# All operands at multiples of 128 bytes in SBUF: a pad behind the constants and wider slots in a two-layer diffusion trunk

## The chip, the cores and the metric

One core of one Trainium2 chip runs the whole kernel as one program. The metric is the device time in microseconds. The profile is one execution, recorded by the hardware profiler.

## The reference

Two layers work on 640 tokens of 1024 features: 128 prompt tokens and 512 latent ones. All data are float32. Each layer is a feed-forward, a mixer and a second feed-forward, each with its modulated norm and a gated residual:

```python
def swiglu(h, w_in, w_out):                      # w_in (1024, 5632), w_out (2816, 1024)
    gt, up = jnp.split(h @ w_in, 2, axis=-1)
    return (jax.nn.silu(gt) * up) @ w_out

def ffn_sublayer(x, mod, g, w_in, w_out, slot):
    h = pre_norm(x, g, mod[:, 3 * slot], mod[:, 3 * slot + 1])
    return x + 0.5 * mod[:, 3 * slot + 2] * swiglu(h, w_in, w_out)

# layer 0: x += gate * concat(conformer_conv(u), hgrn2(u)) @ w_out, u = pre_norm(x) @ w_in
# layer 1: x += gate * windowed attention with a sink logit, QK norm and 2-D rotary
```

The modulation comes from `silu(cond) @ w_mod + b`, with one condition for the prompt tokens and one for the latent ones.

## The kernel before

Activations lie feature-major: `x` is `[128 partitions, 8, 640 tokens]`, so a tile of 128 features is 640 float32 values per partition. The tokens are split in two chunks (`CHUNKS`), first tokens 384 to 639 (256 columns), then tokens 0 to 383 (384 columns).

Every large matrix product is made by `product_steps` (line L531 of the profile). A float32 operand is split into two float32r parts: a rounded one (`hi`, a cast on ScalarE, L517) and the rest (`lo`, a subtraction on VectorE, L518). For each of the contraction's tiles of 128 there are three products, `hi*hi`, `hi*lo` and `lo*hi`, which sum in one PSUM bank. TensorE loads 128 columns of weights for each (LDWEIGHTS, the profile's PEld) and streams 256 or 384 columns of the activations past them (MATMUL).

```python
terms = ((whi, xhi), (whi, xlo), (wlo, xhi))
for j, (a, b) in enumerate(terms):
    self.last_mm = nc.tensor.matmul(ps, lhsT=a[k], rhs=b[k][:, c0:c0 + n], ...
```

In a feed-forward (`ffn`) there are 22 tiles of 128 hidden features, in parts of 8, 8 and 6. A tile takes two products over 8 contraction tiles (gate and value, `pg` and `pu` in the profile), a part ends with a product into the 8 output tiles (`po`, in `project_out`). The mixers use the same routine for their 34 projections (`pj_...`), and their output projection is made in two halves of 4 tiles, with the same `po`; their operand is then called `m`. The attention's scores (L1210, `as`) are float32r products too.

SBUF is given out by pools, one after the other, in this order: the constants (`const`), `x` (`xp`), 6 raw weight tiles (`raw`), 3 + 3 split weight tiles `whi`/`wlo` (`w`), then `slots`, scratch (`tmp`) and `small`. The pool `slots` holds 12 slots of 640 columns, 6 wide ones (`N_WIDE`, 685 columns, for the conv's padded input) and 16 pairs, each of two tiles of 640. The norm's output `h`, the hidden features `g` and the mixers' `m` are pairs, hi and lo side by side; these are the operands that TensorE streams. Weights of the start of the next phase, or of the last output tiles before a norm (`wg`, `wu`, `o` without hi and lo in the profile's names), are split into slots instead, narrow or wide.

Each tile is rounded up to a multiple of 32 bytes per partition, and begins where the one before it ends.

Of the kernel before, what the change touches and what calls it, by code (L numbers as in the profile page):

```python
# [8 lines left out]
F32 = mybir.dt.float32  # L9
# [7 lines left out]
P = 128  # L17
# [3 lines left out]
T = TP + TS  # L21
# [9 lines left out]
WIDE = T + 45  # L31
AHEAD = 400
# [34 lines left out]
class Trunk:  # L67
# [21 lines left out]
    def pair(self, name, dtype=F32):  # L89
        """two tiles of T columns side by side, [P, 2, T], until free(name)"""  # L90
        assert name not in self.held, name
        j = self.free_pairs.pop(0)
        self.held[name] = ("pair", j)
        return self.slots.tile([P, 2, T], dtype, tag=f"pair{j}", name=name)

    def two(self, name, dtype):
        """the two parts of a value"""
        if self.free_pairs:
            t = self.pair(name, dtype)
            return t[:, 0], t[:, 1]  # L100
        self.held[name] = ("two", None)
        return self.slot(f"{name}hi", dtype), self.slot(f"{name}lo", dtype)

    def slot(self, name, dtype=F32, n=T):
        """a tile of T columns until free(name): a slot, or half of a pair; with self.spread_out the one that has been
        free for longest"""
        assert name not in self.held, name
        if n > T:
            j = next(j for j in self.free_slots if j < N_WIDE)
            self.free_slots.remove(j)  # L110
            self.held[name] = ("slot", j)
            return self.slots.tile([P, WIDE], dtype, tag=f"slot{j}", name=name)[:, :n]
        never = float("inf")
        halves = [x for x in self.halves if x[2] == dtype]
        age = {"half": self.freed["half", halves[0][0], halves[0][1]] if halves else never,
               "slot": self.freed["slot", self.free_slots[0]] if self.free_slots else never,
               "pair": self.freed["pair", self.free_pairs[0]] if self.free_pairs else never}
        order = ("slot", "half", "pair")
        if self.spread_out:
            order = sorted(order, key=age.get) if dtype == F32 else ("slot", "half", "pair")  # L120
            if dtype == F32 and len(self.free_slots) <= KEPT:
                order = sorted(("half", "pair"), key=age.get) + ["slot"]
        kind = next(k for k in order if age[k] < never)
        if kind == "slot":
            j = next((j for j in self.free_slots if j >= N_WIDE and not self.spread_out), self.free_slots[0])
            self.free_slots.remove(j)
            self.held[name] = ("slot", j)
            return self.slots.tile([P, WIDE if j < N_WIDE else T], dtype, tag=f"slot{j}", name=name)[:, :n]
        if kind == "half":
            half = halves[0]  # L130
            self.halves.remove(half)
        else:
            j = self.free_pairs.pop(0)
            t = self.slots.tile([P, 2, T], dtype, tag=f"pair{j}", name=name)
            half = (j, 0, dtype, t)
            self.halves.append((j, 1, dtype, t))
            self.freed["half", j, 1] = self.freed["pair", j]
        self.held[name] = ("half", half)
        return half[3][:, half[1], :n]
# [22 lines left out]
    def banks(self, n_mm, n_acc=0, n_mod=0):  # L162
        """the eight PSUM banks: for products, for sums held over several steps, for the modulation, for the rest"""
        n_aux = 8 - n_mm - n_acc - n_mod
        self.bank, b = {}, 0
        for kind, n in (("mod", n_mod), ("mm", n_mm), ("acc", n_acc), ("aux", n_aux)):
            self.bank[kind] = list(range(b, b + n))
            b += n
# [17 lines left out]
    def plan(self, n, points, skip):  # L186
        """the next n fillers go to the next so many points"""
        points -= skip
        self.points = [0] * skip + [-(-n * (p + 1) // points) + (-n * p // points) for p in range(points)]
# [34 lines left out]

    def vec_block(self, b):
# [24 lines left out]
    def transpose_x(self, rows):  # L250
        """x feature-major, and 1 / sqrt(mean square + eps) by token on all partitions"""
# [26 lines left out]
    def conditions(self):  # L278
        """conditions after silu, by feature"""
# [10 lines left out]
    def mod_piece(self, l, slot, q):  # L290
        """256 of the modulation's features; the contraction in four parts that run side by side on columns of the
        array"""
# [18 lines left out]
    def mod_step(self, l, slot, k):  # L311
        """one of eight steps of a whole slot: products with the conditions summed by partition, over the steps by
        VectorE and at the end over the partitions by TensorE, a quarter of the features by part of the array"""
# [51 lines left out]
    def square_into(self, k, c):  # L365
        """squares of a tile summed into acc; the last tiles' stay apart"""
# [17 lines left out]
    def rstd(self, sq_tiles, blocks, scale_col, eps, name, eng=None):  # L384
        """1 / sqrt(mean + eps) by token, tokens on partitions: [P, len(blocks)]; tiles with their first tokens"""
# [16 lines left out]
    def inv_root(self, r, x, scale, name, eng=None):  # L402
        """r = scale / sqrt(x), x > 0: a guess from the exponent, a Newton step and one of third order (1e-9)"""
# [26 lines left out]
    def spread(self, col, out):  # L430
        """a value by token (on partitions) to all partitions: out [P, 128 tokens]"""
        self.nc.tensor.transpose(out, col.to_broadcast([P, P]), self.ident)
# [54 lines left out]
    def split_w_slots(self, raw, name):  # L487
        """the same with the parts in slots, until free(name)"""
# [34 lines left out]
    def product_steps(self, ps, w, x, c0, n):  # L523
        """ps += w.T @ x, float32 operands as exact sums of two float32r parts"""
# [11 lines left out]
    def ffn_first(self, l, which, j):  # L536
        """the weights of a tile of hidden features, for the gate and for the value, with names"""
# [3 lines left out]
    def prefetch(self):  # L541
        """weights of the next phase's start, into slots"""
# [48 lines left out]
    def project_out(self, w, xhi, xlo, n, final, last=False):  # L591
        """x += gate * (w.T @ x); the last tiles before a norm run chunk by chunk, which hides the norm's start"""
# [52 lines left out]
    def root_table(self, after):  # L645
        """has the square root's table loaded ahead"""
# [21 lines left out]
    def project(self, w_ap, name, fine=False):  # L668
        """one tile of 128 features: yields (psum, first token, tokens), and None in between"""
# [11 lines left out]
    def project_tokens(self, w_ap, dst, name):  # L681
        """256 features, token-major, block by block; dst(block): (output, first feature, features) to copy"""
# [18 lines left out]
    def even_constants(self):  # L701
# [20 lines left out]
        # forget gate lb + (1 - lb) * sigmoid(z) as lb_mid + lb_half * tanh(z / 2)  # L722
# [3 lines left out]
        # the conv's gate is 2 * sigmoid(z) = 1 + tanh(z / 2)  # L726
# [3 lines left out]
    def conv_tile(self, ct, w, by_chunk=False):  # L730
        """the gated input of 128 channels: prompt and sample, with 15 zeros before, between and after"""
# [43 lines left out]
    def front(self, ins, n):  # L775
        """counts DVE time; the instruction is one that taps may follow"""
        self.marker = ins
        self.dve_time += n + 60

    def background(self, last=False):  # L780
        """taps for the time that DVE has left while TensorE works on what is emitted so far"""
# [7 lines left out]
    def tick(self):  # L789
        """after a chunk of products: next steps of the scan and of the conv's norm, queued behind them, and taps"""  # L790
# [82 lines left out]
    def hgrn_scan(self, h, qf, gates):  # L873
        """steps of a head's scan"""
# [9 lines left out]
        # scores, transposed: A[s, block, t]; the levels replace all of a block but its diagonal  # L884
# [14 lines left out]
        for lv in range(LEVELS):  # L899
# [3 lines left out]
            def mixed(a, b0, nb):  # L903
                """of pairs of runs of w: the first from a[:, 0] and the second from a[:, 1]"""
# [32 lines left out]
        # states: prompt f, b; sample f after blocks 0..2, b after blocks 3..1  # L937
# [120 lines left out]
    def mix_out(self, w, n, k0, k1, names):  # L1058
        """the part of the output projection that reads tiles k0 to k1 of the mixer's output"""
# [15 lines left out]
    def rope(self, x, name):  # L1075
        """rotates the sample tokens of x in place"""
# [17 lines left out]
    def odd_values(self, w):  # L1094
        """values token-major: prompt, sample blocks 0..3, cache, two blocks in a slot"""
# [7 lines left out]
    def odd_keys(self, w, i, fine=False):  # L1103
        """two heads: parts of the keys, each on both halves of the partitions, for sample blocks 0, 1, the cache
        and sample blocks 2, 3; the prompt's apart"""
# [51 lines left out]
    def head_squares(self, ps, t0, n, r, name):  # L1157
        """mean square + eps by token, for both heads of the 128 features in ps: r[:, 2 * block + head]"""
# [10 lines left out]
    def odd_queries(self, w, i):  # L1169
# [13 lines left out]
        # per head both parts stacked on the partitions: [hi; lo] and [lo; hi]  # L1183
# [9 lines left out]
    # first key column, key columns, first band column, value blocks, by query block  # L1193
# [3 lines left out]
    def attend_scores(self, i, b):  # L1197
        """exp(scores - maximum) of two heads' queries in a block, and the terms of their sums"""
# [33 lines left out]
    def attend_turn(self, i, b):  # L1232
        """keys to the partitions"""
# [32 lines left out]
    def attend_sums(self, i):  # L1266
        """divides by the sums of both heads"""
# [168 lines left out]
```

## Time and profile before

| | us |
|---|---|
| median of 3 runs | 2555.15 (2554.66 to 2556.28) |
| span of the profiled execution | 2550.6 |
| TensorE busy in it | 2503.3 |
| VectorE busy | 1513.1 |
| ScalarE busy | 815.9 |
| GpSimd busy | 193.1 |

The profiled execution's span, from its first to its last instruction, lies 4.6 us below the median of the timed runs; the rest is outside the span. A matmul's record is longer than the distance to the next one, since they are pipelined. Their pace is therefore read from start to start.

### The profile page before, as it was taken

The numbers are of one execution on the slowest core, as the hardware profiler recorded it, in microseconds if no ns is written. First come the engines' busy times: TensorE is split into PE (matmuls) and PEld (weight loads), VectorE is DVE, ScalarE is ACT, GpSimd is POOL, SyncE is SP. The second block draws the span as 40 slices with busy tenths as digits, with TensorE's granted clock in tenths as the row PEclk, the third lists the DMA queues.
The fourth block names the chain that finished last, engine by engine and source line by source line (L and its number), as shares of the span: only waits on it lengthen the run. The fifth ranks groups of instructions, "written<-read, shape, count | busy, mean of one in ns | idle before, by whom it ended". The sixth has DMA issues, their size and how long they took to land. (4 is left out here: it accounts for less than half of the span.)

```text
span 2550.6 us, 42680 instructions
## 1 busy us (share of the span) xinstructions
PE 2503.3 (98%) x17802; PEld 2440.3 (96%) x17802; DVE 1513.1 (59%) x2733; ACT 815.9 (32%) x1519; POOL 193.1 (8%) x282
## 2 busy tenths in 40 slices
PE   8999999999989999999999999999999999999999
PEld 5999999999989999999999999999988899999999
DVE  6765665569987766455556544545667863333333
ACT  5222212443234422221233212223465642222121
POOL 0000000124143000000010000000122010000000
PEclk9999999999999999999999999999999999999999
DMA  8654444311211344344433433433200122222221
GB/s 279 186 157 133 139 143 136 105 53 54 61 32 42 94 124 142 107 133 133 122 103 101 132 108 108 124 106 118 59 19 15 42 84 68 82 75 75 83 63 54
DMA packets 368522, 254.50 MB, mean 100 GB/s; under 512 B 8789, under 2 KB 350152, under 8 KB 368328
## 3 DMA queue, kind: packets, MB, share of 16 engines
q1 hardware_dynamic: 363384, 248.35, 32.3%
q10 hardware_dynamic: 4944, 3.41, 0.4%
q8 instruction: 140, 2.29, 0.4%
q14 instruction: 54, 0.44, 0.1%
HBM read 248.32 MB, written 3.41 MB: 99 GB/s over the span
## 5 line engine op out<-in xcount | busy, mean ns | idle before, releaser
L531 PE MATMUL po<-g,whi_o 128*128 128x256 f32 (+1 forms) x2672 | 573.4, 307 | 0.0
L531 PE MATMUL pg<-h,whi_wg 128*128 128x256 f32 (+1 forms) x2656 | 572.5, 307 | 0.0
L531 PE MATMUL pu<-h,whi_wu 128*128 128x256 f32 (+1 forms) x2656 | 568.2, 306 | 0.3 <-DVE nt L456 0.3
L531 PEld LDWEIGHTS po<-g,whi_o 128*128 128x128 f32 x2672 | 442.7, 188 | 3.7 <-ACT whi_o L517 1.2
L531 PEld LDWEIGHTS pg<-h,whi_wg 128*128 128x128 f32 x2656 | 441.3, 188 | 2.9 <-issue 2.5
L531 PEld LDWEIGHTS pu<-h,whi_wu 128*128 128x128 f32 x2656 | 439.9, 188 | 0.6 <-issue 0.6
L325 DVE SCALAR_TENSOR_TENSOR ma<-raw_wm,cond,ma 128x512 f32<-128x512 f32 x448 | 316.6, 747 | 205.2 <-DMA raw_wm<-in_w_mod 205.1
L531 PE MATMUL po<-g,wlo_o 128*128 128x256 f32 (+1 forms) x1336 | 408.5, 306 | 0.0
L531 PE MATMUL pg<-h,wlo_wg 128*128 128x256 f32 (+1 forms) x1328 | 406.8, 306 | 0.0
L531 PE MATMUL pu<-h,wlo_wu 128*128 128x256 f32 (+1 forms) x1328 | 405.8, 306 | 0.0
L605 DVE SCALAR_TENSOR_TENSOR x<-po,modG,x 128x256 f32<-128x256 f32 (+1 forms) x384 | 156.5, 435 | 240.3 <-PE po L531 239.3
L531 PEld LDWEIGHTS po<-g,wlo_o 128*128 128x128 f32 x1336 | 250.8, 188 | 0.0
L531 PEld LDWEIGHTS pg<-h,wlo_wg 128*128 128x128 f32 x1328 | 250.2, 188 | 0.0
L531 PEld LDWEIGHTS pu<-h,wlo_wu 128*128 128x128 f32 x1328 | 249.3, 188 | 0.0
L517 ACT CAST whi_o<-raw_o 128x1024 fp32r<-128x1024 f32 (+3 forms) x113 | 104.4, 924 | 385.7 <-PE po L531 246.2
L575 DVE TENSOR_TENSOR sil<-sil,pu 128x256 f32<-128x256 f32 (+1 forms) x176 | 85.3, 485 | 204.5 <-PE pu L531 200.7
L517 ACT CAST g<-sil 128x256 fp32r<-128x256 f32 (+1 forms) x176 | 80.4, 457 | 307.7 <-DVE sil L575 307.6
L518 DVE TENSOR_TENSOR wlo_wu<-raw_wu,whi_wu 128x1024 fp32r<-128x1024 f32 x83 | 101.5, 1223 | 119.3 <-ACT whi_wu L517 119.3
L517 ACT CAST whi_wg<-raw_wg 128x1024 fp32r<-128x1024 f32 x83 | 87.3, 1051 | 255.4 <-issue 130.7
L517 ACT CAST whi_wu<-raw_wu 128x1024 fp32r<-128x1024 f32 x83 | 87.2, 1050 | 216.8 <-PE pg L531 167.0
L382 POOL TENSOR_TENSOR acc<-acc,sq 128x256 f32<-128x256 f32 (+1 forms) x44 | 41.9, 954 | 1442.7 <-ACT sq L381 1442.5
L518 DVE TENSOR_TENSOR wlo_o<-raw_o,whi_o 128x1024 fp32r<-128x1024 f32 (+3 forms) x113 | 121.5, 1075 | 30.7 <-ACT whi_o L517 28.6
(412 smaller groups left out, 3470.5 us busy)
## 6 DMA issues: line engine op xcount, KB each, us to landing
raw_wm<-in_w_mod SPq DMA_DIRECT2D x144, 512.0 KB, 3.6
raw_wg<-in_ffn_w_in SPq DMA_DIRECT2D x88, 512.0 KB, 3.8
raw_wu<-in_ffn_w_in SPq DMA_DIRECT2D x88, 512.0 KB, 4.0
raw_o<-in_ffn_w_out SPq DMA_DIRECT2D x64, 512.0 KB, 4.1
raw_o<-in_ffn_w_out SPq DMA_DIRECT2D x32, 384.0 KB, 3.5
raw_z<-in_ev_w_in SPq DMA_DIRECT2D x8, 512.0 KB, 3.8
raw_oq<-in_od_w_in SPq DMA_DIRECT2D x8, 512.0 KB, 3.7
raw_o<-in_od_w_out SPq DMA_DIRECT2D x16, 256.0 KB, 2.7
```

The source lines that it names most:

```text
L325: nc.vector.scalar_tensor_tensor(out=acc, in0=part, scalar=col, in1=acc, op0=ALU.mult, op1=ALU.add)
L382: nc.gpsimd.tensor_tensor(out=self.acc[:, c0:c0 + n], in0=self.acc[:, c0:c0 + n], in1=sq[:, 0:n], op=ALU.add)
L517: nc.scalar.copy(out=hi, in_=src)
L518: nc.vector.tensor_tensor(out=lo, in0=src, in1=hi.bitcast(F32), op=ALU.subtract)
L531: self.last_mm = nc.tensor.matmul(ps, lhsT=a[k], rhs=b[k][:, c0:c0 + n], start=(k == 0 and j == 0), stop=(k == nk - 1 and j == 2))
L575: nc.vector.tensor_tensor(out=s, in0=s, in1=pu, op=ALU.mult)
L605: nc.vector.scalar_tensor_tensor(out=xs, in0=ps[:, s0 - c0:s0 - c0 + sn], scalar=self.modG[:, n, m, g:g + 1], in1=xs, op0=ALU.mult, op1=AL ...
```

## The change

24 float32 values (96 bytes) are given out at the end of the constants and never used. A wide slot becomes 704 columns (2816 bytes) instead of 685 (2740, rounded up to 2752); what is read and written in it stays as long as before. The rest of the difference is blank lines in the place of comments.

```diff
+WIDE_ROOM = 704
...
-            return self.slots.tile([P, WIDE], dtype, tag=f"slot{j}", name=name)[:, :n]
+            return self.slots.tile([P, WIDE_ROOM], dtype, tag=f"slot{j}", name=name)[:, :n]
...
-            return self.slots.tile([P, WIDE if j < N_WIDE else T], dtype, tag=f"slot{j}", name=name)[:, :n]
+            return self.slots.tile([P, WIDE_ROOM if j < N_WIDE else T], dtype, tag=f"slot{j}", name=name)[:, :n]
...
         self.modG = c.tile([P, 6, KD, 2], F32, name="modG")
 
+        c.tile([P, 24], F32, name="pad")
```

No instruction moves on any engine: the rows of both programs are the same, and so are their waits. The first byte per partition of the tiles, in the two built programs, modulo 128:

| tiles | before | after |
|---|---|---|
| `ident` (streamed in transposes) | 0 | 0 |
| `x`, `raw`, `whi`, `wlo`, 12 narrow slots, scratch | 32 | 0 |
| 6 wide slots | 32, 96, 32, 96, 32, 96 | 0 |
| 16 pairs (`h`, `g`, `m`) | 96 | 0 |

A tile of 128 weight columns is 512 bytes, a pair's half 2560 and the first chunk's start inside a tile 1536 bytes, all of them multiples of 128. So an operand of a product has the remainder of its tile.

## Rows read from the trace of the kernel before

**Rows 1.** The page's first part: busy us (share of the span) x instructions.
```profile
PE 2503.3 (98%) x17802; PEld 2440.3 (96%) x17802; DVE 1513.1 (59%) x2733; ACT 815.9 (32%) x1519; POOL 193.1 (8%) x282
```

**Rows 2.** The waits: engine, line, what released it: us in total, times, longest.
```profile
PE hgb L432 <- DVE r_hg L414: 9.9, 3, 6.4
...
DVE x L605 <- PE po L531: 239.3, 139, 3.7
```

**Rows 3.** Stretches A:B of the span, line L531 alone: busy us (instructions), clock, DMA.
```profile
100.00:480.00 380.00, 373.25 (x2579) 370.30 (x2578) 1.00 0.46 140
...
1340.00:1790.00 450.00, 444.59 (x3084) 441.99 (x3083) 1.00 0.38 115
```

**Rows 4.** Order in time, TensorE, first feed-forward: start us, us, line, tiles, count.
```profile
300.51 0.51 PE L531 MATMUL pg<-h,whi_wg 128*128 128x384 f32 x2
300.86 0.34 PE L531 MATMUL pg<-h,wlo_wg 128*128 128x384 f32 x1
301.03 0.51 PE L531 MATMUL pg<-h,whi_wg 128*128 128x384 f32 x2
301.38 0.34 PE L531 MATMUL pg<-h,wlo_wg 128*128 128x384 f32 x1
301.55 0.51 PE L531 MATMUL pg<-h,whi_wg 128*128 128x384 f32 x2
301.90 0.34 PE L531 MATMUL pg<-h,wlo_wg 128*128 128x384 f32 x1
302.07 0.51 PE L531 MATMUL pu<-h,whi_wu 128*128 128x384 f32 x2
```

**Rows 5.** Order in time, TensorE, 256 columns in the same stage.
```profile
306.23 0.39 PE L531 MATMUL pg<-h,whi_wg 128*128 128x256 f32 x2
...
307.25 0.39 PE L531 MATMUL pg<-h,whi_wg 128*128 128x256 f32 x2
```

**Rows 6.** Order in time, TensorE: transposes of the scan, products of the conv's norm.
```profile
611.38 1.04 PE L950 MATMUL kt<-ident,k 128*128 128x128 f32 x8
...
748.91 1.84 PE L815 MATMUL cmu<-cw,ones_c 128*128 128x399 f32 x5
```

**Rows 7.** The same lines' views: duration ns min/median/max, first and last start, forms.
```profile
L950 PE MATMUL kt<-ident,k x32: 270/272/273, 611.4 to 823.7; 128*128 128x128 f32 x32
...
L815 PE MATMUL cmu<-cw,ones_c x16: 377/440/501, 746.5 to 756.3; 128*128 128x399 f32 x8, 128*128 128x256 f32 x8
```

**Rows 8.** Order in time, TensorE, attention scores.
```profile
1875.75 0.33 PE L1210 MATMUL as<-khi,qs 128*128 128x384 f32 x1
...
1876.46 0.34 PE L531 MATMUL pj_oq<-h,whi_oq 128*128 128x384 f32 x1
...
2021.97 0.34 PE L1210 MATMUL as<-khi,qs 128*128 128x384 f32 x1
...
2022.67 0.50 PE L531 MATMUL po<-m,whi_o 128*128 128x384 f32 x2
```

**Rows 9.** Order in time, TensorE, a norm's sums: one column streamed.
```profile
510.89 0.58 PE L391 MATMUL rs_n<-ones_d,apart 128*128 128x1 f32 x4
511.33 0.36 PE L391 MATMUL rs_n<-ones_d,acc 128*128 128x1 f32 x2
511.56 0.47 PE L391 MATMUL rs_n<-ones_d,apart 128*128 128x1 f32 x3
```

**Rows 10.** Order in time, TensorE, output tiles after the even mixer, two windows.
```profile
853.42 0.76 PE L531 MATMUL po<-m,o 128*128 128x256 f32 x5
...
854.02 0.75 PE L531 MATMUL po<-m,o 128*128 128x256 f32 x5
```

**Rows 11.** Order in time, TensorE, a projection of the even mixer.
```profile
539.98 0.40 PE L531 MATMUL pj_q<-h,whi_q 128*128 128x256 f32 x2
...
541.04 0.40 PE L531 MATMUL pj_q<-h,whi_q 128*128 128x256 f32 x2
...
541.39 0.52 PE L531 MATMUL pj_q<-h,whi_q 128*128 128x384 f32 x2
...
542.45 0.34 PE L531 MATMUL pj_q<-h,whi_q 128*128 128x384 f32 x1
```

## The prediction

> **What bounds the kernel.** I read the page's engine totals first: TensorE is busy for 2503.3 of 2550.6 us, VectorE for 59% and ScalarE for 32% [rows 1]. The reader is to see that no other engine comes near the span. The waits say the same from the other side: TensorE's longest is for VectorE, 9.9 us in three places, while VectorE waited 239.3 us for one kind of product alone [rows 2]. So only TensorE's own pace can move the time by much. A shorter ScalarE, VectorE or GpSimd instruction, or a faster transfer, would be hidden.
>
> Next I read what TensorE does with its time. Line L531, the float32r products, fills 373.25 of 380 us and 444.59 of 450 in two feed-forward stages, at a granted clock of 1.00 [rows 3]. From the code there are 7536 products of 384 columns and as many of 256: per chunk 4 feed-forward layers x (22 tiles x 2 x 24 + 8 tiles x 66) = 6336, the mixers' 34 projections x 24 = 816, and their output projections 2 x 192 = 384.
>
> The third view is the order in time, for the distance from start to start (a product's own length overlaps the next one). From 300.51 to 302.07 us there are nine products of 384 columns: 1.56 / 9 = 173.3 ns each [rows 4]. From 306.23 to 307.25 there are nine of 256: 113.3 ns [rows 5]. [...]
>
> [...]
>
> **The change, part by part.** It adds no instruction, takes none away and moves none: in the built programs all five engines' instructions, with their waits, stand in the same order. The pad is a tile that nothing writes. The wider slots are read with the old lengths. What changes is addresses alone. Both operands of the products go from 32 mod 64 to 0 mod 64, and the streamed operand (pairs, 96 before) and the weights (32 before), which lay in opposite 64-byte halves of a 128-byte stretch, now lie in the same one.
>
> - ScalarE, VectorE, GpSimd and transfers: nothing, and if something, then hidden behind the waits of [rows 2]. The price without that cover would be any slowdown of VectorE beyond its idle 41%.
> - [...] In the attention scores both operands are at 32: four products of 384 from 2021.97 to 2022.67 us are 175.0 ns each, four from 1875.75 to 1876.46 are 177.5 [rows 8]. That is 1.7 to 4.2 ns more, 13 to 32 us in all.
> - [...] The next weights are loaded meanwhile, and where a product streams one column only, six come in 510.89 to 511.56 us, 111.7 ns each [rows 9]: that is the weight load by itself. [...] The loss: the weights of the fifth output tile after the even mixer (o1_4) lie at 96, like the operand they meet, and five products take 853.42 to 854.02 us, 120.0 ns each [rows 10]; 6.7 x 7536 = 50 us.
>
> I take the gain, nearly whole: 83 + 12 = 95 us. [...] The profiled execution lasts 2550.6 us, 4.6 below the median of 2555.15; what lies around the span stays. 2555 - 95 = **2460 us**, between 2440 (83 + 32) and 2505 (50).
>
> [...]
>
> **Rivals.**
> - *Nothing happens.* [...] Against it: [rows 10], where an address alone changes the pace. Time: 2555. [...]
> - *Slower, by weights and stream in the same half.* Before, the halves were opposite in nearly all products; afterwards they are the same in all. If the start does not count and only the meeting of the two does, the 256-column products go to between 117 and 120 ns and the 384-column ones to between 173.3 and 177.5. Price: 7536 x 3.7 = 28 us to 50 + 32 = 82 us, so 2583 to 2637, in the middle 2610. [...] For it: [rows 8, 10] show it. Against it: the same opposite halves already run at two paces. From 539.98 to 541.04 us nine products of 256 take 117.8 ns, and from 541.39 to 542.45 six of 384 take 176.7 [rows 11], with the addresses of [rows 4, 5] modulo 512; so 120.0 may be little more than this slower rhythm.
> [...]
> - *The change doesn't do what it says.* In the built program x, the raw weights, the split weights, all slots, all pairs and the scratch tiles begin at multiples of 128, and the chunks begin 1536 bytes inside them, so I rule it out.
>
> **How the numbers follow.** A measurement of this kernel can tell 0.2%, 5 us, from no change. The gain has 0.53, with 2460 in it the likeliest and 2440 to 2505 its own range. No change within 5 us has 0.20; I give it less than the plain reading would, because a changed meeting of stream and weights should shift the rhythm a little even if the start is worth nothing. Slower has 0.27. The range goes from 2435 to 2595: it holds the gain but for its tail, no change, and of the slower case the part in which little more than the 256-column products suffer; about 0.2 is left out, nearly all of it above.
>
> **What would show it.** Right: nine products of 384 columns in a feed-forward stage in about 1.46 us, not 1.56, nine of 256 in about 1.00, VectorE's and ScalarE's durations unchanged, their idle time shorter, and TensorE still busy for 98%. Half right: 384 at about 166.7 ns, 256 at 113.3. Wrong: 173.3 and 113.3 again (start without effect), or 256 at 117 to 120 throughout (same half). It would also be wrong if TensorE got faster and then waited: VectorE is busy for 59% of the span [rows 1], so I do not expect that.

## The result and the profile after

The changed kernel takes 2591.01 us (median of 4 runs, 2589.73 to 2596.21), against 2554.9 of the kernel before (now 4 runs): a ratio of 1.0147 [1.0135, 1.0159]. It is 36 us slower, where 95 us less were forecast. The profiled execution has a span of 2590.2 us.

The page's first part (engine, busy us, share of the span, instructions):

```profile
PE 2543.9 (98%) x17802; PEld 2480.5 (96%) x17802; DVE 1515.0 (58%) x2733; ACT 816.2 (32%) x1519; POOL 192.1 (7%) x282
```

Against [rows 1] TensorE is busy 40.6 us longer, and the span is 39.6 us longer. VectorE, ScalarE and GpSimd stay within 2 us of their old totals. So the loss is TensorE's own work. The waits (engine, line, what released it: us in total, times, longest) say the same:

```profile
DVE x L608 <- PE po L534: 253.5, 145, 3.7
...
PE hgb L435 <- DVE r_hg L417: 10.3, 3, 6.2
```

TensorE waits as little as in [rows 2] (10.3 us, 9.9 before), and VectorE waits for it a little more (253.5 us, 239.3 before). L534 and L608 are the old L531 and L605.

The stretches of two feed-forward stages, the product line alone (busy us, instructions, clock, DMA), show the same busy time with fewer products in it:

```profile
100.00:480.00 380.00, 373.26 (x2523) 370.32 (x2523) 1.00 0.47 137
1365.00:1815.00 450.00, 445.62 (x3024) 443.54 (x3025) 1.00 0.38 112
```

In [rows 3] the first stretch had 2579 products, here it has 2523, at the same granted clock of 1.00. The busy time for each product went from 373.25 / 2579 = 144.7 ns to 373.26 / 2523 = 147.9. Which width it is, the order in time shows (start us, us, line, tiles, count):

```profile
306.89 0.51 PE L534 MATMUL pu<-h,whi_wu 128*128 128x384 f32 x2
...
311.05 0.40 PE L534 MATMUL pg<-h,whi_wg 128*128 128x256 f32 x2
...
316.80 0.51 PE L534 MATMUL pg<-h,whi_wg 128*128 128x384 f32 x2
```

A tile takes 24 products per chunk. From 306.89 to 311.05 there are 24 of 384 columns, 173.3 ns each, as in [rows 4]. From 311.05 to 316.80 there are 48 of 256 columns, 119.8 ns each; [rows 5] had 113.3. Summed from start to start over every product of the line, the 256-column ones took 898.2 us before and 936.4 after, the 384-column ones 1336.8 and 1338.6. That is 40.0 us more, and all but 1.8 of it belongs to the narrow chunk.

### The profile page after: what moved, and what is told of

It reads as the page before. It is cut to its first block, busy times and chain, and to the rows that moved or that the text cites. A ratio compares the mean times of both kernels' runs of the same rounds, so it can differ in the third digit from the quotient of the medians.

```text
span 2590.2 us, 42680 instructions
## 1 busy us (share of the span) xinstructions
PE 2543.9 (98%) x17802; PEld 2480.5 (96%) x17802; DVE 1515.0 (58%) x2733; ACT 816.2 (32%) x1519; POOL 192.1 (7%) x282
## 5 line engine op out<-in xcount | busy, mean ns | idle before, releaser
L534 PE MATMUL po<-g,whi_o 128*128 128x256 f32 (+1 forms) x2672 | 584.4, 310 | 0.0
L534 PE MATMUL pg<-h,whi_wg 128*128 128x256 f32 (+1 forms) x2656 | 583.3, 309 | 0.0
L534 PE MATMUL pu<-h,whi_wu 128*128 128x256 f32 (+1 forms) x2656 | 580.0, 309 | 0.3 <-DVE nt L459 0.3
L534 PEld LDWEIGHTS po<-g,whi_o 128*128 128x128 f32 x2672 | 448.7, 189 | 3.7 <-ACT whi_o L520 1.2
L534 PEld LDWEIGHTS pg<-h,whi_wg 128*128 128x128 f32 x2656 | 447.5, 190 | 2.9 <-issue 2.5
L534 PEld LDWEIGHTS pu<-h,whi_wu 128*128 128x128 f32 x2656 | 447.0, 190 | 0.6 <-issue 0.6
L534 PE MATMUL po<-g,wlo_o 128*128 128x256 f32 (+1 forms) x1336 | 412.0, 308 | 0.0
L534 PE MATMUL pg<-h,wlo_wg 128*128 128x256 f32 (+1 forms) x1328 | 410.3, 309 | 0.0
L534 PE MATMUL pu<-h,wlo_wu 128*128 128x256 f32 (+1 forms) x1328 | 409.7, 308 | 0.0
L608 DVE SCALAR_TENSOR_TENSOR x<-po,modG,x 128x256 f32<-128x256 f32 (+1 forms) x384 | 156.8, 435 | 254.5 <-PE po L534 253.5
L534 PEld LDWEIGHTS po<-g,wlo_o 128*128 128x128 f32 x1336 | 252.8, 189 | 0.0
L534 PEld LDWEIGHTS pg<-h,wlo_wg 128*128 128x128 f32 x1328 | 252.1, 190 | 0.0
L534 PEld LDWEIGHTS pu<-h,wlo_wu 128*128 128x128 f32 x1328 | 252.0, 190 | 0.0
```

What stands on the lines that cost most here:

```text
L608: nc.vector.scalar_tensor_tensor(out=xs, in0=ps[:, s0 - c0:s0 - c0 + sn], scalar=self.modG[:, n, m, g:g + 1], in1=xs, op0=ALU.mult, op1=AL ...
```

## The experiments

The built programs gave the quantity to look at. It is called the distance here: the first byte per partition of the streamed operand minus that of the weights, modulo 256. Weights begin at byte 67616 before and 67712 after (96 more, the pad), the first pair at 136672 and 137088 (416 more: the pad, and 64 for each of the five wide slots ahead of the pairs). So the distance goes from 192 (in 14,974 of the 15,072 products) to 0 (in all). In the other 98, with weights in slots, it was 0, 64 or 128. The pad moves both operands alike, the wide slots move only the pairs.

The expectations name theories by letters. M: weights and stream in the same half of a 128-byte stretch. S: the start of the operands alone. P: the places of other tiles. D: the distance, with a longer period than 128. H: the place inside 64 bytes. For the last pair of runs, W: the loading of the weights is slowed only while something streams; F: a fixed price for each product; L: the stream is slowed too.

All shifts are one unused tile ahead of the first pair, so the pairs and what lies behind them move, against the weights, `x` and the raw tiles ahead of them. The edit, here 64 bytes on the changed kernel (`opp64`):

```diff
-        self.held = {}
+        self.held, self.shifted = {}, False
...
+        if not self.shifted:
+            self.shifted = True
+            self.slots.tile([P, 16], F32, tag="shift", name="shift")
```

**Run opp64** (after, pairs + 64 bytes: opposite halves, starts still at multiples of 64).

> The changed kernel with 64 more bytes ahead of the pairs: weights stay at 0 modulo 128, the streamed operands go from 0 to 64. Theory M (the meeting counts: streamed operand and weights in the same 64-byte half of a 128-byte stretch slow the 256-column products): back to 113.3 ns for most of them, 384 columns at 173.3, time 2550 to 2558. Rival S (the start of the weights counts: at a multiple of 128 their load is slower than at 32): 119.7 ns stays, 2591. Rival P (the other tiles' places count, x, raw weights, scratch): nearly all of them stay where the change put them, so 2591. [...]

2576.03 us, 1.0091 [1.0076, 1.0106]. Moving the pairs gives back 15 of the 36 us, so the meeting matters; but it is not the time of before, although the halves are opposite again. M by itself falls, and so do S and P, which both had 2591. Order in time, TensorE:

```profile
341.88 0.51 PE L537 MATMUL po<-g,whi_o 128*128 128x384 f32 x2
...
346.05 0.40 PE L537 MATMUL po<-g,whi_o 128*128 128x256 f32 x2
...
348.87 0.51 PE L537 MATMUL po<-g,whi_o 128*128 128x384 f32 x2
```

24 products of 256 columns in 2.82 us are 117.5 ns each; 384 columns stay at 4.17 / 24 = 173.8.

**Run same32** (before, pairs + 64 bytes: same half, starts still at 32 mod 64).

```diff
+            self.slots.tile([P, 16], F32, tag="shift", name="shift")
```

> The kernel before with 64 more bytes ahead of the pairs: streamed operands at 32 modulo 128 instead of 96, weights at 32 as before, nothing at a multiple of 64. Theory M: same half, so 256 columns at about 119.7 ns, 384 at 173.4, time 2588 to 2595, as with the change. Rival S: weights at 32 as before, so 113.3 ns and 2555. Rival P: other tiles as before, so 2555.

2592.11 us, 1.015 [1.0135, 1.0165]. The kernel before is made as slow as the changed one with no start at a multiple of 64. S and P, which both had 2555, fall here too.

**Runs d32 and d96** (after, pairs + 32 and + 96 bytes).

```diff
+            self.slots.tile([P, 8], F32, tag="shift", name="shift")
```

> The changed kernel with 32 more bytes ahead of the pairs: weights at 0, streamed operands at 32 modulo 128, so half of each 64-byte piece of the one lies in the other's half. Theory M, if the halves are sharp: both kinds of start fall in the same half, 119.7 ns and 2591; if it goes by distance: between, about 116.5 ns and 2572. Rival S: weights at 0, 119.7 ns, 2591. Rival P: 2591.

```diff
+            self.slots.tile([P, 24], F32, tag="shift", name="shift")
```

> The changed kernel with 96 more bytes ahead of the pairs: weights at 0, streamed operands at 96 modulo 128. Theory M, if the halves are sharp: opposite halves, 113.3 ns and 2555; if it goes by distance: between, about 116.5 ns and 2572. Rival S: 119.7 ns, 2591. Rival P: 2591. It also shows whether any distance is better than that of the kernel before (64).

d32: 2582.15 us, 1.0121 [1.0099, 1.0142]; d96: 2610.77, 1.0226 [1.0211, 1.0242]. By M d96, whose halves are opposite, should be the faster of the two; it is 29 us slower. In d96 the wide chunk suffers too (order in time, TensorE):

```profile
344.93 0.40 PE L537 MATMUL po<-g,whi_o 128*128 128x256 f32 x2
...
347.81 0.52 PE L537 MATMUL po<-g,whi_o 128*128 128x384 f32 x2
...
352.05 0.40 PE L537 MATMUL po<-g,whi_o 128*128 128x256 f32 x2
```

2.88 / 24 = 120.0 ns for 256 columns, 4.24 / 24 = 176.7 for 384.

**Run a192** (after, pairs + 192 bytes: the distance of before, all starts at multiples of 64).

```diff
+            self.slots.tile([P, 48], F32, tag="shift", name="shift")
```

> The changed kernel with 192 more bytes ahead of the pairs: weights at 0 and streamed operands at 64 modulo 128, as in the run with 64 bytes (256 columns at 117.7 ns, 2576), but the distance from weights to stream modulo 512 is 448, as in the kernel before. Theory D (the distance counts, modulo 256 or 512): 113.3 ns and 2555. Theory H (the place within 64 bytes counts as well; starts at 32 keep the better pace, starts at 0 do not): 117.7 ns and 2576.

2550.74 us, 0.9988 [0.9979, 0.9998]. This speaks for D against the rest: the whole loss is gone with the pad, the wide slots and the even starts all in place. Against the kernel before, with the same distance and uneven starts, 3 us are gained, which is inside the 0.2% that can be told from no change.

**Runs b128, b32 and b96** (before, pairs + 128, + 32 and + 96 bytes).

```diff
+            self.slots.tile([P, 32], F32, tag="shift", name="shift")
```

> The kernel before with 128 more bytes ahead of the pairs: starts modulo 128 as before (stream 96, weights 32), but the distance modulo 512 is 64, as in the run of the changed kernel with 64 bytes. Theory D: 117.7 ns and 2576. Theory H: 113.3 ns and 2555.

```diff
+            self.slots.tile([P, 8], F32, tag="shift", name="shift")
```

> The kernel before with 32 more bytes ahead of the pairs: weights at 32, streamed operands at 0 modulo 128, distance 96. Theory D by distance alone: as the changed kernel with 96 bytes, about 120 ns for 256 columns, 177 for 384, 2611. [...]

```diff
+            self.slots.tile([P, 24], F32, tag="shift", name="shift")
```

> The kernel before with 96 more bytes ahead of the pairs: weights at 32, streamed operands at 64 modulo 128, distance 32. Theory D by distance alone: as the changed kernel with 32 bytes, about 117.5 ns for 256 columns, 174.8 for 384, 2582. [...]

b128: 2576.17 us, 1.0089 [1.007, 1.0108]; b32: 2584.37, 1.0118 [1.01, 1.0137]; b96: 2585.88, 1.0127 [1.0106, 1.0147]. b128 has the distance of opp64 (64) and its time within 0.2 us, though all starts differ by 32 bytes and the distances differ by 256; b96 has that of d32 (32) and its time within 4. H falls, and a period of 256 is enough at these two distances and at 0 (same32 and the changed kernel, also 256 apart). For b32 the expectation under D, 2611, missed by 27 us: it took the distance as 96, which holds modulo 128 alone. Modulo 256 it is 224, not timed until then. So the period is not 128.

**Runs pad_only and wide_only** (the two halves of the change, each alone).

```diff
+        c.tile([P, 24], F32, name="pad")
```

> One part of the change alone: the 96 bytes behind the constants, wide slots as before. Weights go to 0, streamed operands to 64 modulo 128, the distance from weights to stream stays 192 modulo 256. Theory D (only the distance modulo 256 counts): 113.3 ns for 256 columns, 2550 to 2558. Theory H (the start counts too): slower, about 2576.

```diff
-            return self.slots.tile([P, WIDE], dtype, tag=f"slot{j}", name=name)[:, :n]
+            return self.slots.tile([P, 704], dtype, tag=f"slot{j}", name=name)[:, :n]
...
-            return self.slots.tile([P, WIDE if j < N_WIDE else T], dtype, tag=f"slot{j}", name=name)[:, :n]
+            return self.slots.tile([P, 704 if j < N_WIDE else T], dtype, tag=f"slot{j}", name=name)[:, :n]
```

> The other part alone: wide slots of 2816 bytes, constants as before. All starts stay at 32 modulo 64, the distance goes from 192 to 0 modulo 256. Theory D: the whole loss, 119.7 ns for 256 columns, 2588 to 2595. Theory H: no operand begins at a multiple of 64, so 2555.

pad_only: 2560.74 us, 1.0024 [1.0015, 1.0033]; wide_only: 2591.74, 1.0145 [1.0127, 1.0163]. The wide slots alone are the whole loss, at starts of 32 mod 64 as before. The pad alone, which puts the weights and the streamed operands at multiples of 64, gains nothing: it is 6 us slower, 3 us above the range that was expected for it. Order in time, TensorE, of pad_only and then of wide_only:

```profile
343.59 0.39 PE L532 MATMUL po<-g,whi_o 128*128 128x256 f32 x2
...
346.31 0.51 PE L532 MATMUL po<-g,whi_o 128*128 128x384 f32 x2
...
350.47 0.39 PE L532 MATMUL po<-g,whi_o 128*128 128x256 f32 x2
```

```profile
340.54 0.40 PE L531 MATMUL po<-g,whi_o 128*128 128x256 f32 x2
...
343.41 0.51 PE L531 MATMUL po<-g,whi_o 128*128 128x384 f32 x2
...
347.58 0.40 PE L531 MATMUL po<-g,whi_o 128*128 128x256 f32 x2
```

24 products of 256 columns take 2.72 us with the pad (113.3 ns each) and 2.87 us with the wide slots (119.6); 384 columns take 4.16 and 4.17 us (173.3 and 173.8). The 6 us are in the products all the same: summed over the line, pad_only has 6.2 us more in those of 256 columns and 3.1 us more in those of 384 than the kernel before. The part of its narrow products that come 117 to 119 ns apart is 20%, against 11% before and 9% in a192. They come in whole stretches of the span: 78% of the line's products between 1100 and 1200 us run at the slower pace of their width, under 1% between 1200 and 1300.

**Runs a128 and a160** (after, pairs + 128 and + 160 bytes: the two distances still missing).

```diff
+            self.slots.tile([P, 32], F32, tag="shift", name="shift")
```

> The changed kernel with 128 more bytes ahead of the pairs: distance 128 modulo 256, a value not seen yet. Theory D with a period of 256: open, between 2550 and 2611. Theory D with a period of 128 (all starts at 0 as in the change): 119.7 ns, 2591.

```diff
+            self.slots.tile([P, 40], F32, tag="shift", name="shift")
```

> The changed kernel with 160 more bytes ahead of the pairs: distance 160 modulo 256, the last of the eight places in steps of 32 bytes. Theory D: open, between 2540 and 2611; below 2550 it would beat the kernel before.

a128: 2603.27 us, 1.0191 [1.0176, 1.0206]; a160: 2590.81, 1.0138 [1.012, 1.0156]. a128 is 12 us slower than the changed kernel's 2591, so the period is not 128 here either. With them all eight distances that tiles rounded to 32 bytes allow are timed. The two columns of ns are means from start to start, over the products of the line that stand between two of the same width; gaps of 200 ns and more, under 1% of them, are left out:

| distance | runs, ratio to before | 256 columns, ns | 384 columns, ns |
|---|---|---|---|
| 192 | before; a192 0.9988; pad_only 1.0024 | 113.9 to 114.4 | 173.6 to 174.0 |
| 64 | opp64 1.0091; b128 1.0089 | 117.7 | 173.4 |
| 32 | d32 1.0121; b96 1.0127 | 117.2, 117.3 | 174.6, 175.0 |
| 224 | b32 1.0118 | 118.3 | 173.5 |
| 160 | a160 1.0138 | 118.3 | 174.5 |
| 0 | after 1.0147; same32 1.015; wide_only 1.0145 | 119.6 | 173.5 |
| 128 | a128 1.0191 | 118.7 | 176.0 |
| 96 | d96 1.0226 | 120.0 | 176.6 |

The fourteen programs are put into groups by the distance alone. Four of the groups hold two or three programs. At the distances 64, 32 and 0 these have different starts, and their times agree within 0.1%. At 192 a192 and pad_only are 0.4% apart, with intervals that do not meet, though even their starts agree modulo 512. The other four groups hold one program each.

**Runs c512_before and c512_after** (chunks of 128 and 512 columns in place of 256 and 384, with the addresses of before and of after). They were to show which of the two is held up, the loading of the weights or the stream.

```diff
-CH = 384
+CH = 512
```

> The kernel before with chunks of 128 and 512 columns instead of 256 and 384 (distance 192). Theory W (a product lasts as long as the longer of its stream and the next weights' load, and only the load suffers from the meeting): 128 columns are bound by the load, about 112 ns, 512 by the stream, 226 to 231 ns; time about 2555 + 7536 x (112 + 229 - 113.3 - 173.3) = 2960, between 2900 and 3020.

> The changed kernel with the same chunks of 128 and 512 columns (distance 0). Theory W: the stream of 128 columns ends after about 60 ns, the rest of the load runs undisturbed, so 128 columns cost at most 4 ns more than with the addresses of before, 512 columns the same; the two versions differ by 0 to 30 us. Rival F (each product of the shorter chunk pays a fixed 6 ns for the meeting, whatever its width): 48 us more than with the addresses of before. Rival L (the longer the two run side by side, the more is lost, stream included): 512 columns slower by 6 ns or more, 50 to 100 us.

c512_before: 3120.4 us, 1.2217 [1.2199, 1.2235]; c512_after: 3091.56, 1.2118 [1.2098, 1.2138]. All three theories missed: with these chunks the changed addresses are faster, by 29 us, where they had 0 to 100 us slower. The 60 ns for a stream of 128 columns are an estimate; from [rows 5] to [rows 4] 128 columns more take 173.3 - 113.3 = 60.0 ns. Order in time, TensorE, of c512_before and then of c512_after:

```profile
1150.67 0.63 PE L531 MATMUL pu<-h,whi_wu 128*128 128x512 f32 x2
...
1156.27 0.33 PE L531 MATMUL pg<-h,whi_wg 128*128 128x128 f32 x2
...
1158.89 0.39 PE L531 MATMUL pu<-h,whi_wu 128*128 128x128 f32 x2
...
1161.57 0.68 PE L531 MATMUL pg<-h,whi_wg 128*128 128x512 f32 x2
```

```profile
1151.64 0.39 PE L534 MATMUL pu<-h,whi_wu 128*128 128x128 f32 x2
...
1154.32 0.69 PE L534 MATMUL pg<-h,whi_wg 128*128 128x512 f32 x2
...
1159.87 0.62 PE L534 MATMUL pu<-h,whi_wu 128*128 128x512 f32 x2
...
1165.31 0.33 PE L534 MATMUL pg<-h,whi_wg 128*128 128x128 f32 x2
```

24 products of 512 columns take 5.60 us with the distance 192 (233.3 ns each). With the distance 0 the two sets shown take 5.55 and 5.44 us (231.3 and 226.7). Over the whole line the means are 233.3 and 228.1 ns, without gaps of 300 ns and more. 24 of 128 columns take 2.68 us with either, 111.7 ns each (2.62 us in the other set of c512_before), the pace that [rows 9] have with one column. Summed over the line, the 512-column products took 1828.0 us and 1791.7 (4.8 ns less each), the 128-column ones 926.4 and 933.5: 29.2 us less in all, against 30.7 of the two spans.

Both times are also 130 to 160 us above the 2960 us or so that was expected. In some stretches TensorE does less, and its granted clock is lower, as the first of these two of c512_before shows (columns as above, the product line alone):

```profile
1000.00:1100.00 100.00, 76.03 (x355) 63.63 (x355) 0.81 0.24 70
1100.00:1200.00 100.00, 100.00 (x581) 86.85 (x580) 1.00 0.37 107
```

Why they do less stays open; the paces of the sets above are from stretches with a granted clock of 1.00.

## Why the prediction was wrong

The time, 2591, lies inside the stated range of 2435 to 2595, but that is no merit of the forecast of 2460: the range was drawn wide to take in its rivals, and the kernel moved the other way.

- **TensorE is the only bound**: right. No other engine's total moved by more than 2 us, and the 40 us of span are in its products.
- **The change moves addresses alone**: right, but the prediction read them modulo 128 and tile by tile. What counts is a difference of two addresses, modulo 256, and in this reading the change gives up the best of eight distances.
- **384 columns, the gain of 83 us**: here the forecast failed. No run shows the pace behind it, 162.3 ns (173.3 less 83 us / 7536); the lowest mean at any of the eight distances is 173.4. Nor does any show that of the weak end, 50 us or 166.7 ns. pad_only and a192 have starts at multiples of 64 with the old distance, and mean paces of 113.9 to 114.4 and 173.6 to 174.0 ns, as before: the even start saved nothing. In its place the distance showed: from 192 to 0 it costs the narrow products 5.6 ns (114.0 to 119.6) and the wide ones nothing (173.6 to 173.5).
- **256 columns, the gain of 12 us**: it is an estimate, 7536 x (113.3 - 111.7), down to the pace of [rows 9]. It did not come either: no distance has a mean below 113.9. The 32 us of the strong end have no pace in any run behind them.
- **"[rows 10], where an address alone changes the pace"**: they show less. Their 120.0 ns were set against 113.3 of another stage. The products just ahead of them, with weights at the distance 192, already come at about 117 ns (order in time, TensorE, before):

```profile
852.36 0.52 PE L531 MATMUL po<-m,o 128*128 128x256 f32 x3
...
853.18 0.52 PE L531 MATMUL po<-m,o 128*128 128x256 f32 x3
```

  Seven take the 0.82 us from 852.36 to 853.18 (117.1 ns), the next seven the 0.84 us to 854.02 (120.0). So the address of these weights is worth some 2 to 3 ns there, not 6.7.
- **The rival "slower, by weights and stream in the same half"**: its direction and its price for the narrow chunk were right. It gave 117 to 120 ns; measured are 119.6. Its condition was too coarse: opp64 has opposite halves and is at 117.5. In the built program the five products of [rows 10] have the distance 0, which is that of the changed kernel, and their 120.0 ns are its pace for 256 columns. Its price for 384 columns, from [rows 8], was too high: the attention scores also have the distance 0, at 175.0 to 177.5, but the products of the line stay at 173.5. With 5.6 ns (119.6 - 114.0) for 7536 products this rival's sum would have been 42 us; the narrow products' sum from start to start grew by 38.2.
- **The objection that before ran at two paces** [rows 11]: the two rhythms are real. At the distance 192, 9 to 20% of the narrow products come 117 to 119 ns apart in the kernel before, a192 and pad_only. This is a part of why less than 6.7 x 7536 = 50 us is lost: a tenth of before was slow already. The rest is on the other side, where 19% of the narrow products of the changed kernel stay at 116 to 119 ns. What sets off the slower rhythm stays open, and with it the 0.4% between a192 and pad_only.
- **The rival "nothing happens"**: right for the pad, wrong for the wide slots. In pad_only the starts go from 32 mod 64 to 0, and the paces stay at 113.3 and 173.3 ns, though its ratio of 1.0024 [1.0015, 1.0033] is a little above 1. With the whole change the time did not stay at 2555; wide_only has all of that loss at starts of 32 mod 64.

Shown is that the distance between the pairs and what lies ahead of them decides whether the 36 us are lost, by runs that take the loss away from the changed kernel and bring it into the kernel before. It does not settle the last 0.4%. All shifts move the pairs against the weights, `x` and the raw tiles by the same amount, so these runs alone do not single out the weights. The two lines above from the stage of [rows 10] do speak for them: there only the place of the weights differs. In the trace the first product at 120 ns is the last one ahead of the o1_4 weights, and the last of o1_4 is at 118 again, as if the stream met the load of the next product's weights; that is one place. That load and stream get in each other's way is the author's guess; it is not shown, and no run shows which of them is held up. The last two runs speak against the weights as the only ones that pay: at 512 columns the pace, 226.7 to 233.3 ns, is over twice the 111.7 of [rows 9], and the distance still matters, the other way round. This stays open.

No version beats the kernel before by more than can be told from no change; its distance is the best of the eight for its chunks.

## What to carry to other kernels

Where a kernel is bound by float32r products, as this one is, print the addresses of weights and streamed operands in the built program and look at their difference modulo 256, before and after any edit of the pools: a few bytes in a tile that no product touches can cost 1 to 2% (1.0118 for the 32 bytes of b32, 1.015 for the 64 of same32). Alignment of all operands to 64 or 128 bytes is worth nothing by itself here (a192 0.9988, pad_only 1.0024, the changed kernel 1.0147). Multiples of 128 leave only the differences 0 and 128, with ratios of 1.0147 and 1.0191; 0 was also the better of the two tried for chunks of 128 and 512 columns (3091.56 us, 3120.4 with 192). Move the operands against each other with an unused tile, time all eight places, and do it again when the width of the products changes.

## What the runs showed of the hardware that was not expected

At two of the distances the time from start to start, at a granted clock of 1.00, grows evenly with the width. At the distance 0 it is 120.0 ns for 256 columns (78% of these products of the changed kernel come 120 ns apart), 173.3 for 384 (93% at 173 or 174) and, in the second set of c512_after, 226.7 for 512: 53.3 ns more for each 128 columns. At the distance 192 it is 113.3 and 173.3 ns, and 233.3 for 512 columns in c512_before: 60.0 ns more for each 128. So the two distances tie at 384 columns, which is why the wide chunk of this kernel did not notice the change, and they change places at 512.

These paces are no rule for the rest. In c512_before the products of 512 columns come mostly 230 to 231 or 235 to 236 ns apart, which only in the mean is 233.3. At the distance 64 those of 256 columns are mostly at 117 and 118 ns, between the two paces above. And the attention scores of 512 columns have the distance 0 in the kernel before as well, but mostly come 224 to 236 ns apart there. So something besides the distance sets the pace, and no run here shows what.
